# A matmul operand at another place modulo 256 bytes, and unread products in the first wait

## The chip, the cores and the metric

One core of a Trainium2 chip runs the whole program. The metric is the device time of one execution in microseconds (us); lower is better. Six names recur: TensorE (PE, and PEld for its loads of the stationary operand), VectorE (DVE), ScalarE (ACT), GpSimd (POOL), SyncE (SP, which issues most DMAs), and the DMA queues. "Stationary" is the operand that a matmul holds (128 x 128 here), "moving" the one that streams past it.

## What is computed

A trunk of four layers on x, 512 rows of 1024 numbers in float32. Each layer adds a mixer and then an FFN to x, both behind an RMS norm; the mixers are S5 (layers 0 and 3), gated linear attention (1) and differential attention (2). What the change touches most is the FFN, which is the same in all four layers:

```python
def swiglu_ffn(h, w_gate_up, w_down):
    g, u = jnp.split(h @ w_gate_up, 2, axis=-1)
    return (jax.nn.silu(g) * u) @ w_down
...
x = x + swiglu_ffn(h, ffn_w_gate_up[layer], ffn_w_down[layer]).astype(x.dtype)
```

h has 512 rows and 1024 columns, w_gate_up 2 x 2816 columns, w_down is 2816 x 1024.

## The kernel before

**Products in parts.** A float32 operand is split into a high part that TensorE takes in one pass (float32r) and a low rest. ScalarE rounds the high part (L404), VectorE subtracts it (L412), and a product is three single-pass matmuls: high with high, high with low, low with high. The weights' parts lie in the buffers "whl" (pool wp, five buffers of 8192 bytes in each partition).

**The FFN's first half.** The 2816 hidden columns are worked in 11 blocks of 256 (`seven_block`, L580). A block's gate and up columns are computed together with h in the manner of Strassen: seven products of half-size matrices in place of eight. Each product (`seven_product`, L565, its matmul at L575) is 24 matmuls: 2 halves of the output x 4 parts of the contraction x 3 parts. The weights are stationary (128 x 128 from whl), and a "side" of h is moving (256 columns at a time). A side is a tile of 2 x 4 x 256 numbers, 8192 bytes in a partition, made once in each layer: "11", "12", "1", "2", "3", "4" and "22". The steps and their sides and banks are: one (side 11, bank a), five (1, c), six (2, a), two (12, d), seven (3, a), three (4, c), four (22, a). Two is the only one with bank d, which comes from `sbank` (tag "s"); a and c come from `acc`.

**Where the sides lie.** `Sides.room` (L160) takes a tile "sides" of 4096 + 64 numbers from the pool hp (tag hT, two buffers, 16640 and 16384 bytes) and places "11" at number 48 and "12" at number 2112 of it. The other five are tiles of the FFN's own pool (`Sides.open`). The pool wp with whl lies right behind hp. Lines `self.edge(pool, n)` add tiles of n bytes that nothing uses.

**The order in the FFN** (`ffn`, L721). First an opening: blocks 0 and 1 (called a and b) run step by step in an order written out by hand, `plan`, in which the sides are made as well. Then groups: nb blocks, each one, five, six, two, seven, three, four, and behind them the second half, `gemm_b` twice (d = 0, 1), in which the blocks' results ("act") are stationary and w_down's columns move, 512 at a time (L432 to L434). Groups have 4, 4 and 3 blocks in layers 1, 2 and 3, and 3, 3, 3 and 2 in layer 0; the opening's blocks 0 and 1 belong to the first group. In layers 0 and 1 small pieces of other work (`job`) are put between the matmuls of `gemm_b`.

**The kernel's start** (`s5_first`, L1594). The first S5 mixer's tables are computed on VectorE from small inputs while x arrives. TensorE has little to do: it transposes the parameters (L920, L935), then waits for a DMA (craw) for L1141, `s5_qt`, whose result cps VectorE takes at L1160. Behind it stands `warmed(12)`: twelve full-precision products of ident with itself into a bank that nobody reads, which keep TensorE busy until the next transposes (L1038) can run. From the line `self.hand(PE, Activation)` on, the order on TensorE and ScalarE is that of the code. zT, the tile of the mixer's turned outputs, lies idle until the first of them is written.

Of the kernel before, what the change touches and what calls it, by code (L numbers as in the profile page):

```python
# [11 lines left out]
F32 = mybir.dt.float32  # L12
# [9 lines left out]
P = 128  # L22
# [45 lines left out]
class Left:  # L68
# [15 lines left out]
    def room(self):  # L84
        self.hT = [self.tr.hp.tile([P, KT, SEQ], F32R, tag="hT", name=f"hT{z}") for z in range(2)]
# [67 lines left out]
class Sides(Left):  # L153
# [6 lines left out]
    def room(self):  # L160
        F = self.tr.hp.tile([P, 4, 4, 256], F32, tag="hT", name="halves")
        self.whole = F
        self.F = {(0, 0): F[:, 0], (1, 0): F[:, 1], (0, 1): F[:, 2], (1, 1): F[:, 3]}

        two = self.tr.hp.tile([P, 4096 + 64], F32R, tag="hT", name="sides")
        at = lambda n: two[:, n : n + 2048].rearrange("p (z k n) -> p z k n", z=2, k=4)
        self.place = {"11": at(48), "12": at(2112)}
        self.heads = []

    def quarter(self, q, half, b):  # L170
# [154 lines left out]
class Trunk:  # L325
# [254 lines left out]
    def seven_block(self, fp, slots, left, wgu, b, turn, na):  # L580
# [48 lines left out]
        def room1(room=None):  # L629
            load("1", 0, 1, (0, 0), room)  # L630

        def room22(room=None):
            load("22", 1, 1, None, room)
# [87 lines left out]
    def ffn(self, l, left, after=None, turn=False, aside=None, small=None):  # L721
# [7 lines left out]
        with self.tc.tile_pool(name=f"ffn{l}", bufs=1, reuse_waits="tile") as fp:  # L729
# [6 lines left out]
            if glued:  # L736
                lent = room()
# [448 lines left out]
            else:  # L1186
                self.dq.dma_start(d[r, :, g], src[r])

    def warmed(self, n):

        ps = self.sbank("warmed")
        for _ in range(n):
            self.nc.tensor.matmul(ps[:, :P], self.ident[:], self.ident[:], start=True, stop=True)

    def s5_rows(self, nb, bp, Q):

# [397 lines left out]
    def s5_first(self, ctx):  # L1594
        nc, i = self.nc, self.i
        xin = self.xp.tile([P, NT, D], F32, tag="x", name="xin")
        zpool = ctx.enter_context(self.tc.tile_pool(name="zT0", bufs=1, side="right"))
        zT = zpool.tile([P, 2, KT, SEQ], F32R, name="zT")
        self.edge(zpool, 32)
        with self.tc.tile_pool(name="s5_0", bufs=1) as p:  # L1600
            scr, more = (self.hp.tile([P, 4096], F32, tag="hT", name=f"scr{z}") for z in range(2))
            oms = [more[:, 1024 * z : 1024 * z + 1024].rearrange("p (a b) -> p a b", a=2) for z in range(2)]
# [33 lines left out]
            with self.tc.issue_after(self.last_power.ins):  # L1636
                new_x(0)
                X[0][2]()
            self.hand(mybir.EngineType.PE, mybir.EngineType.Activation)
            with self.tc.issue_after(self.last_sine.ins):  # L1640
                ps = self.s5_qt(raw[0][1])
                self.warmed(12)
                hu = self.s5_in(scr, xin, (rounded, rows[0]))
            with self.tc.issue_after(self.last_row.ins):
                X[0][3]()
# [6 lines left out]
            room = [four[:, n] for n in range(4)] + [wide[:, 512:], self.np_.tile([P, 512], F32, tag="R", name="z1", bufs=1)[:]]  # L1652
# [851 lines left out]
```

## Time and profile before

| what | value |
|---|---|
| timed runs, median of 3 | 2278.27 us (2277.72 to 2279.32) |
| the profiled execution, first to last instruction (span) | 2272.3 us |
| granted TensorE clock, mean | 0.996 |

The profile is one execution, taken by the hardware profiler; its page gives the span and no other time of that execution. "Busy" of a group is the time in which at least one of its instructions ran. Matmuls overlap: the mean length of one includes its way through the array, so the pace of a stream is read from where the next one starts. "x24" counts instructions; a full-precision product counts as two matmuls, and a single-pass one as one.

### The profile page before, as it was taken

What the parts mean: (1) busy time and instruction counts of PE and PEld (TensorE: products, weight loads), DVE (VectorE), ACT (ScalarE), POOL (GpSimd) and SP (SyncE); (2) the same over time, 40 slices, a digit from 0 to 9 for tenths busy, and PEclk for the clock granted to TensorE, in tenths of its full rate; (3) what the DMA queues carried; (4) which work ended last, traced back from release to release, by engine and by line L of the source; (5) the groups of instructions that cost most, each with busy time, mean ns of one, the idle gap of its engine ahead of it and who ended that gap; (6) DMA issues with size and microseconds to landing.
All of it is one profiled execution on the core that took longest, in us unless ns stands there. A gap on an engine that the chain in (4) does not pass through costs nothing. (4 is left out here: it accounts for less than half of the span.)

```text
span 2272.3 us, 37257 instructions
## 1 busy us (share of the span) xinstructions
PE 2198.1 (97%) x14871; PEld 1955.4 (86%) x14871; DVE 1584.4 (70%) x2413; ACT 1109.9 (49%) x1779; POOL 328.0 (14%) x446
## 2 busy tenths in 40 slices
PE   6999999999999999999999999999999899999998
PEld 5888889889777799998988887999999888989997
DVE  9965878786525488777745676976766965957675
ACT  6634545454443355554435675644534224635343
POOL 6401142421000010100002231110000000101000
PEclk9999999999999999999999999999999999999999
DMA  4356666663322556665247465985641555766622
GB/s 88 64 171 167 166 157 179 163 180 93 114 76 66 153 154 177 181 172 154 94 139 149 98 148 135 230 213 143 170 100 57 141 155 147 194 172 157 168 75 75
DMA packets 294504, 319.92 MB, mean 141 GB/s; under 512 B 70141, under 2 KB 233241, under 8 KB 294202
## 3 DMA queue, kind: packets, MB, share of 16 engines
q1 hardware_dynamic: 231706, 235.79, 34.1%
q0 software_dynamic: 62624, 81.75, 19.4%
q8 instruction: 117, 1.92, 0.3%
q14 instruction: 57, 0.47, 0.1%
HBM read 285.62 MB, written 16.65 MB: 133 GB/s over the span
## 5 line engine op out<-in xcount | busy, mean ns | idle before, releaser
L412 DVE TENSOR_TENSOR whl<-wst,whl 128x1024 fp32r<-128x1024 f32 x272 | 331.9, 1225 | 267.7 <-ACT whl L404 267.0
L404 ACT CAST whl<-wst 128x1024 fp32r<-128x1024 f32 x272 | 284.5, 1051 | 342.5 <-PE acc L434 242.2
L575 PE MATMUL a<-side,whl 128*128 128x256 f32 x3168 | 383.0, 277 | 6.7 <-DVE whl L412 6.0
L575 PEld LDWEIGHTS a<-side,whl 128*128 128x128 f32 x3168 | 370.2, 188 | 8.9 <-DVE whl L412 6.8
L432 PE MATMUL acc<-whl,act 128*128 128x512 f32 x704 | 278.9, 396 | 1.8 <-DVE g L620 1.6
L433 PE MATMUL acc<-whl,act 128*128 128x512 f32 x704 | 275.7, 392 | 0.0
L434 PE MATMUL acc<-whl,act 128*128 128x512 f32 x704 | 275.7, 392 | 0.0
L575 PE MATMUL c<-side,whl 128*128 128x256 f32 x2112 | 254.8, 277 | 3.6 <-DVE whl L412 3.6
L575 PEld LDWEIGHTS c<-side,whl 128*128 128x128 f32 x2112 | 246.6, 188 | 4.5 <-DVE whl L412 4.4
L412 DVE TENSOR_TENSOR whl<-slot,whl 128x1024 fp32r<-128x1024 f32 x105 | 127.9, 1222 | 64.2 <-ACT whl L404 64.1
L432 PEld LDWEIGHTS acc<-whl,act 128*128 128x128 f32 x704 | 132.6, 188 | 31.7 <-DVE g L620 2.0
L434 PEld LDWEIGHTS acc<-whl,act 128*128 128x128 f32 x704 | 132.5, 188 | 27.9
L433 PEld LDWEIGHTS acc<-whl,act 128*128 128x128 f32 x704 | 132.7, 189 | 26.2 <-issue 0.2
L404 ACT CAST whl<-slot 128x1024 fp32r<-128x1024 f32 x105 | 109.9, 1051 | 74.1 <-PE acc L434 28.2
L432 PE MATMUL acc<-whl,hT 128*128 128x512 f32 x352 | 142.1, 404 | 1.5 <-DVE ro L2233 1.5
L434 PE MATMUL acc<-whl,hT 128*128 128x512 f32 x352 | 137.6, 391 | 0.0
L433 PE MATMUL acc<-whl,hT 128*128 128x512 f32 x352 | 137.4, 390 | 0.0
L575 PE MATMUL d<-sides,whl 128*128 128x256 f32 x1056 | 133.6, 283 | 2.6 <-ACT whl L404 2.6
L575 PEld LDWEIGHTS d<-sides,whl 128*128 128x128 f32 x1056 | 128.9, 191 | 3.4 <-ACT whl L404 3.4
L575 PE MATMUL a<-sides,whl 128*128 128x256 f32 x1056 | 128.9, 278 | 1.7 <-DVE whl L412 1.2
L575 PEld LDWEIGHTS a<-sides,whl 128*128 128x128 f32 x1056 | 124.6, 188 | 3.0 <-DVE whl L412 1.4
L611 POOL DMA_DIRECT2D wst<-in_ffn_w_gate_up_dram x44 | 57.1, 1297 | 442.8 <-DMA wst<-in_ffn_w_gate_up_dram 159.6
(458 smaller groups left out, 3930.0 us busy)
## 6 DMA issues: line engine op xcount, KB each, us to landing
wst<-in_ffn_w_gate_up_dram SPq DMA_DIRECT2D x88, 512.0 KB, 4.4
wst<-in_ffn_w_down_dram SPq DMA_DIRECT2D x88, 512.0 KB, 4.4
slot<-in_ffn_w_gate_up_dram SPq DMA_DIRECT2D x69, 512.0 KB, 6.1
wst<-in_ffn_w_gate_up_dram POOLq DMA_DIRECT2D x44, 512.0 KB, 6.0
halves<-in_ffn_w_gate_up_dram SPq DMA_DIRECT2D x42, 512.0 KB, 5.6
wst<-in_s_w_glu_dram SPq DMA_DIRECT2D x32, 512.0 KB, 4.9
wst<-in_gla_w_in_dram SPq DMA_DIRECT2D x24, 512.0 KB, 3.6
wst<-in_diff_w_qkv_dram SPq DMA_DIRECT2D x24, 512.0 KB, 3.7
```

The costliest lines, as they stand in the source:

```text
L404: self.last["high"] = self.nc.scalar.copy(hl[:, 0], w[:])
L412: self.last["low"] = self.nc.vector.tensor_tensor(hl[:, 1], w[:], hl[:, 0].bitcast(F32), op=ALU.subtract)
L432: mm(out, lh, rh, start=first, stop=False)
L433: mm(out, lh, rl, start=False, stop=False)
L434: self.last["mm"] = mm(out, ll, rh, start=False, stop=last)
L575: mm(o, hl[:, x, k, c], side[:, y, k], start=first and not (j or k or n), stop=k == 3 and n == 2, skip_group_check=True,)
L611: nc.gpsimd.dma_start(w[:], left.quarter(*plus, b), accum_op=ALU.add)
```

## The change

The side "12" begins at number 2096 of the tile "sides" and no longer at 2112; its size and everything that reads or writes it stay. `warmed` gets other products and another place: it runs ahead of `s5_qt` (and no longer behind it), with 14 products of ident, then single-pass products with the stationary operand at 16 places (three products of 256 columns at each, steps of 4 numbers) and at 8 places (three of 512 columns, steps of 8 numbers), all read from zT, whose first 1024 numbers GpSimd sets to zero ahead of the tables. Nobody reads the results.

```diff
-        self.place = {"11": at(48), "12": at(2112)}
+        self.place = {"11": at(48), "12": at(2096)}
...
-    def warmed(self, n):
-
+    def warmed(self, room):
+
+        mm = self.nc.tensor.matmul
         ps = self.sbank("warmed")
-        for _ in range(n):
-            self.nc.tensor.matmul(ps[:, :P], self.ident[:], self.ident[:], start=True, stop=True)
+        for _ in range(14):
+            mm(ps[:, :P], self.ident[:], self.ident[:], start=True, stop=True)
+        for n, step in ((256, 4), (512, 8)):
+            for at in range(512, 576, step):
+                for _ in range(3):
+                    mm(ps[:, :n], room[:, at : at + P], room[:, :n], start=True, stop=True)
...
         self.edge(zpool, 32)
+        unread = zT[:].rearrange("p z k n -> p (z k n)")
+        nc.gpsimd.memset(unread[:, :1024].bitcast(F32), 0.0)
         with self.tc.tile_pool(name="s5_0", bufs=1) as p:
...
             self.hand(mybir.EngineType.PE, mybir.EngineType.Activation)
+            self.warmed(unread)
             with self.tc.issue_after(self.last_sine.ins):
                 ps = self.s5_qt(raw[0][1])
-                self.warmed(12)
                 hu = self.s5_in(scr, xin, (rounded, rows[0]))
```

## The prediction

> **What bounds it.** I read the page's busy times and groups first, then the chain of work that ended last inside one FFN, then stretches of TensorE's products.
>
> ```profile
> PE 2198.1 (97%) x14871; PEld 1955.4 (86%) x14871; DVE 1584.4 (70%) x2413; ACT 1109.9 (49%) x1779; POOL 328.0 (14%) x446
> ...
> L575 PE MATMUL d<-sides,whl 128*128 128x256 f32 x1056 | 133.6, 283 | 2.6 <-ACT whl L404 2.6
> ...
> L575 PE MATMUL a<-sides,whl 128*128 128x256 f32 x1056 | 128.9, 278 | 1.7 <-DVE whl L412 1.2
> ```
>
> TensorE is busy nearly all the time, and its FFN products hardly wait: 2.6 us of idle time stand before all 1056 matmuls of the second product (the only one that writes a bank d). The first product reads the same tile "sides" with the same shapes, yet d is busy 4.7 us longer. Why, the chain shows. Columns: start, length, what; one product is 24 matmuls. This is a group of four blocks of layer 2's FFN, in the order one, five, six, two, seven, three, four, and so on:
>
> ```profile
> 1552.95 2.83 PE a L575 x24
> 1555.78 2.83 PE c L575 x24
> 1558.60 2.83 PE a L575 x24
> 1561.43 2.87 PE d L575 x24
> 1564.30 2.74 PE a L575 x24
> 1567.04 2.72 PE c L575 x24
> 1569.76 5.44 PE a L575 x48
> ...
> 1580.64 2.86 PE d L575 x24
> ```
>
> Two things are to be seen. Each d costs 2.86 where the others cost 2.72 (5.44 for two): 0.14 lost, and 0.02 more in the product behind it (2.74). And the first three products of this group do not run at 2.72 but at 2.83, each of them, until the first d (2.87); behind it the pace is 2.72 for good. So there are two stable paces for the same work on the same places, and d, slow itself, is what brings TensorE from the slow one to the fast one. The next view has the first three products (72 matmuls) of all nine such groups: stretch, length, then busy time of PE. At the fast pace they are 3 x 2.72 = 8.16.
>
> ```profile
> 325.58:333.87 8.29, 8.29 (x73) 8.29 (x73) 1.00 0.70 149
> 424.79:432.97 8.18, 8.18 (x73) 8.18 (x72) 1.00 0.94 169
> 523.39:531.87 8.48, 8.48 (x73) 8.48 (x72) 1.00 0.41 132
> 932.56:940.82 8.26, 8.26 (x72) 8.26 (x73) 1.00 0.65 131
> 1053.43:1061.91 8.48, 8.47 (x72) 8.47 (x72) 1.00 0.36 116
> 1552.79:1561.27 8.48, 8.48 (x73) 8.48 (x72) 1.00 0.72 161
> 1673.45:1681.93 8.48, 8.48 (x72) 8.47 (x72) 1.00 0.36 115
> 2053.44:2061.92 8.48, 8.48 (x72) 8.48 (x72) 1.00 0.69 153
> 2174.11:2182.59 8.48, 8.48 (x73) 8.48 (x72) 1.00 0.37 117
> ```
>
> Six groups enter slow (8.48, which is 3 x 2.827) and hold it through all 72 matmuls; three enter fast after a short settling (8.18 to 8.29).
>
> **The place.** Counted from the sizes in the code, "sides" begins at the same place modulo 256 as the weight buffers whl, which lie 16640 + 16384 = 129 x 256 bytes behind it. "11" is 48 x 4 = 192 bytes on, "12" 2112 x 4 = 33 x 256, so 0 on. Counted in the same way, the five other sides are 192 on, side 1 for one: 68800 = 268 x 256 + 192 bytes behind whl. After the change "12" begins at 2096 x 4 = 32 x 256 + 192: at the distance of the six others. In a group that runs fast, two then costs 2.72 like one: 0.14 + 0.02 = 0.16 less for each block. In a group that enters slow, nothing is left that differs from what held 2.83 for three products over three different sides, so I let the slow pace hold to the group's last product.
>
> For a group of n blocks the cost above 7n x 2.72 is now 3 x 0.107 + 0.15 + 0.02 + (n - 1) x 0.16, and then 7n x 0.107. For n = 4 (at 1552 and 2053): 0.97 becomes 3.00, +2.03. For n = 3 (1053, 1673, 2174): 0.81 becomes 2.25, +1.44. For n = 2 (523): 0.65 becomes 1.50, +0.85. Sum: 2 x 2.03 + 3 x 1.44 + 0.85 = +9.2 us. The three fast groups (10 blocks: 3, 3 and 4) give 10 x 0.16 = -1.6. Five blocks that are done before these groups, behind the last wait of a layer's opening (one in layer 0, two in 1 and 3), give -0.8.
>
> What part of this is on the path? In the chain nothing stands between a group's products, so theirs is whole. The openings (a layer's first two blocks) wait for the splits of weights:
>
> ```profile
> 252.93 5.50 PE L575 MATMUL a<-side,whl 128*128 128x256 f32 x46 [1.74 <-DVE whl L412]
> 262.48 2.86 PE L575 MATMUL c<-side,whl 128*128 128x256 f32 x22 [1.10 <-DVE whl L412]
> 932.56 2.98 PE L575 MATMUL a<-sides,whl 128*128 128x256 f32 x24 [0.45 <-DVE x L558]
> 1500.98 2.21 PE L575 MATMUL a<-side,whl 128*128 128x256 f32 x17 [0.43 <-ACT r L679]
> ```
>
> What two:a and two:b save there, some 2 x 0.14 + 0.02 = 0.3 in each layer, ends in a longer wait of this kind: nothing, and -1.2 for all four layers if that cover is gone. In the same way layer 1's 0.32 of the five blocks ends in the wait at 932.56, and layer 2's blocks 2 and 3 in that at 1500.98. So -0.8 becomes -0.5, and the place is worth 9.2 - 1.6 - 0.5 = +7.1 us.
>
> Here a page speaks against any effect. The Trainium skill, "TensorE: Matmul & The Clock Gate", section "Step-by-step: what each phase is for", says that the two operands come through read ports of their own, so that loading the next weights takes nothing from the running matmul. By that the place of a side is worth 0 and the time stays; 2.86 against 2.72 in this trace does not agree.
>
> **The first wait.** Columns: start, length, engine and line; in brackets the idle time before.
>
> ```profile
> 1.45 0.94 POOL L1016 MEMSET frow<- 128x1024 f32 x1
> 4.65 0.24 POOL L991 IOTA params<- 128x128 int32 x1 [2.26 <-PE s5ps L920]
> 5.16 0.30 PE L935 MATMUL s5ps<-ident,params 24*128 24x24 f32 x1 [0.58 <-DVE params L929]
> 15.98 1.12 PE L1141 MATMUL cps<-ident,craw 128*64 128x128 f32 x8 [10.53 <-DMA craw<-in_s_c_re_dram]
> 18.49 4.73 PE L1193 MATMUL warmed<-ident 128*128 128x128 f32 x24
> 23.36 0.60 PE L1038 MATMUL frow<-ident,params 128*12 128x128 f32 x4
> 24.16 0.27 DVE L1160 TENSOR_SCALAR Q<-cps 64x128 f32<-64x128 f32 x1
> 24.29 0.56 ACT L1039 CAST frow<-frow 12x512 fp32r<-12x512 f32 x1
> 42.71 1.09 PE L1141 MATMUL cps<-ident,craw 128*64 128x128 f32 x16
> ```
> ```profile
> 18.48:22.27 3.79, 3.78 (x17) 3.79 (x18) 1.00 0.00 0
> ```
>
> The added memset has the shape of frow's, 0.94, and lies in GpSimd's idle 2.26. The products move ahead of cps (two times 8 records at 15.98 and 17.43): they can start at 5.5. One product on ident is two records; the first 17 here took 3.79, 0.22 each, the remaining seven 0.95 in all with the last one's drain, so about a half each: TensorE comes to its full clock at about 22.3, 6.3 us after its first matmul at 15.98. Taken over: from 5.5 to 11.8 at half speed, which does 3.1 of the work; the work at full speed is 28 x 0.11 + 48 x 0.113 + 24 x 0.227 = 14.0 (0.227 is twice a fast 256). It ends at 11.8 + 10.9 = 22.7, and cps, 1.1 at full clock, at 23.8. frow's four transposes then come 0.45 late, to 24.4, where ScalarE takes them at 24.29; VectorE takes cps at 24.16, and is busy without a break from there to the clip at 30.28. Cost: 0. Bounds: all at full clock from the start ends at 19.5 and gains nothing, as VectorE sets the pace; all at half speed ends at 5.5 + 28 = 33.5, cps at 35.8, and costs 11.6. I take 0, as the clock did rise in this trace after 6.3 us of such work. The Trainium skill, same page, section "The HAM clock gate", has it rise after a busy window of about 3.4 us that runs freely, so after 3.4 to 6.8; this trace's 6.3 agrees, and the sum stays 0.
>
> **Sum.** +7.1 + 0 on the profiled execution's span of 2272.3 gives 2279.4. The page has no other time of that execution; the median of the timed runs, 2278.27, lies 6.0 above its span. Forecast: 2285.4, 0.31% slower.
>
> **Rivals.** (1) The slow pace ends without the old d: in the first two, or in seven, three or four, which were never seen to enter from it. For it: d always left the fast pace behind. Against: the slow pace never ended by itself in 6 x 72 matmuls. Then only the gains count: 3.1 in the six groups ((0.97 - 0.32) x 2 + 0.49 x 3 + 0.33) and 2.1 elsewhere, -5.2: 2273.1; 2271.2 if the six slow entries (0.32 each) go too. This is the faster side; it is decided at one place, the fourth product of a slow group: if two runs at 2.72 there, the sum turns round. (2) The place is not the cause. d is also the only product whose bank has the tag "s"; then nothing changes: 2278.3. Against it stands a product into a bank with that tag, alo, which runs like one into an acc bank (both 391 ns):
>
> ```profile
> L1938 PE MATMUL alo<-hT,walr 128*32 128x512 f32 x16 | 3.8, 391 | 0.0
> ```
> ```profile
> L434 PE MATMUL acc<-whl,hT 128*128 128x512 f32 x352 | 137.6, 391 | 0.0
> ```
>
> The page's rule of separate ports comes to the same time. (3) The slow pace holds in some groups only: between 2274 and 2284. (4) Worse: the slow pace goes over into the 512-wide matmuls behind it (48 for each block, 19 blocks). At the same ratio, 2.83 to 2.72, 0.227 would be 0.236: 19 x 48 x 0.009 = +8, 2293. Against it: these came out at one pace after every 256-wide stretch here. A clock that stays low through the first wait ends near it as well, 2297.
>
> **Numbers.** Forecast 0.62, its own range 2283.1 (the openings' 1.2 and layer 1's 0.3 not hidden, and 0.8, the spread of the timed runs) to 2288.9 (a fast group of three blocks enters slow, 0.48 + 2.25, and the same spread); (1) 0.18; (2) 0.06; (3) 0.06; (4) 0.08. A measurement of this kernel tells about 0.2%, 4.6 us, from no change. Slower by more: 0.62 + 0.08 + 0.02 of (3) = 0.72; within: 0.06 + 0.04 = 0.10; faster: 0.18. The range leaves out most of (4) and the lower half of (1): 2273 to 2290.
>
> **What would show it.** Right: d at 2.72 in the groups at 325, 424 and 932; 2.83 for each of the 28 products of the group at 1552, and d no longer told apart from its neighbours; the six entries at 8.48; VectorE's Q at 24.2 within 0.5. Wrong: 2.72 behind the first two of a slow group (rival 1), 2.86 left at d (rival 2), steps over 0.23 in L432 to L434 behind a slow group (rival 4), cps after 24.2.

## The result, and the profile after

| | before | after |
|---|---|---|
| timed runs, median of 5 each | 2278.27 us (2276.39 to 2279.85) | 2293.92 us (2289.18 to 2295.86) |
| ratio after to before | | 1.0063, 95% interval 1.0050 to 1.0075 |
| the profiled execution, span | 2272.3 us | 2294.1 us |
| first FFN product of layer 0 begins in it | 216.28 us | 221.79 us |

The change costs 15.65 us (the interval: 11.4 to 17.1), more than twice the forecast's 7.1. The two profiled executions lie further apart than the medians (21.8 us), so a size is taken from the timed runs below and a mechanism from the traces.

The page of the kernel after, busy times and groups of the FFN's products (columns as in the prediction):

```profile
PE 2227.2 (97%) x14947; PEld 1983.2 (86%) x14947; DVE 1584.9 (69%) x2413; ACT 1110.6 (48%) x1779; POOL 327.7 (14%) x447
...
L575 PE MATMUL a<-side,whl 128*128 128x256 f32 x3168 | 391.5, 280 | 8.3 <-DVE whl L412 5.9
...
L575 PE MATMUL a<-sides,whl 128*128 128x256 f32 x1056 | 131.4, 281 | 2.0 <-DVE whl L412 1.2
L575 PE MATMUL d<-sides,whl 128*128 128x256 f32 x1056 | 130.4, 280 | 2.5 <-ACT whl L404 2.5
```

The same rows of before that the prediction did not need are these:

```profile
L575 PE MATMUL a<-side,whl 128*128 128x256 f32 x3168 | 383.0, 277 | 6.7 <-DVE whl L412 6.0
```

d went from 133.6 to 130.4 us: the place did make it faster. But the first product over the same tile (a from sides) went from 128.9 to 131.4 and the three products a over other sides from 383.0 to 391.5, although nothing of theirs was touched and the idle time ahead of them hardly moved. The chain of work inside a group of layer 3 shows how (start, length, what):

```profile
2074.82 2.83 PE c L575 x24
2077.65 2.83 PE a L575 x24
2080.48 2.83 PE d L575 x24
2083.30 2.83 PE a L575 x24
```

d is no longer told apart, and the product behind it, at which before came to 2.72, runs on at 2.83. The first three products of four of the nine groups of after, in the view that the prediction shows of before (stretch, length, busy PE, busy PEld, clock, DMA share, GB/s):

```profile
330.70:339.28 8.58, 8.58 (x72) 8.58 (x73) 1.00 0.76 157
431.58:439.75 8.17, 8.17 (x72) 8.17 (x72) 1.00 0.93 167
...
943.14:951.70 8.56, 8.56 (x73) 8.56 (x73) 1.00 0.65 132
...
2071.84:2080.32 8.48, 8.48 (x73) 8.48 (x73) 1.00 0.71 153
...
```

The six groups that were forecast slow are slow (8.48 each; one of them is shown). Two more are: the group at 330.70 (8.58, in before 8.29) and the one at 943.14 (8.56, in before 8.26). Only the one at 431.58 is fast. By the order of the products' starts, each slow group keeps 2.83 to its last product, and so do parts of two openings, ten products of layer 1 in one row among them (10 x 2.72 would be 27.20):

```profile
870.01:898.28 28.27, 28.27 (x242) 28.23 (x240) 1.00 0.80 212
```

### The profile page after: what moved, and what is told of

Same layout as the page of the kernel before. It is cut to its first block, busy times and chain, and to the rows that moved or that the text cites. A ratio compares the mean times of both kernels' runs of the same rounds, so it can differ in the third digit from the quotient of the medians.

```text
span 2294.1 us, 37410 instructions
## 1 busy us (share of the span) xinstructions
PE 2227.2 (97%) x14947; PEld 1983.2 (86%) x14947; DVE 1584.9 (69%) x2413; ACT 1110.6 (48%) x1779; POOL 327.7 (14%) x447
## 5 line engine op out<-in xcount | busy, mean ns | idle before, releaser
L575 PE MATMUL a<-side,whl 128*128 128x256 f32 x3168 | 391.5, 280 | 8.3 <-DVE whl L412 5.9
L575 PEld LDWEIGHTS a<-side,whl 128*128 128x128 f32 x3168 | 378.2, 189 | 10.5 <-DVE whl L412 6.7
L432 PE MATMUL acc<-whl,act 128*128 128x512 f32 x704 | 277.9, 395 | 1.2 <-DVE g L620 1.2
L434 PE MATMUL acc<-whl,act 128*128 128x512 f32 x704 | 274.7, 390 | 0.0
L575 PE MATMUL c<-side,whl 128*128 128x256 f32 x2112 | 260.2, 280 | 3.3 <-DVE whl L412 3.3
L575 PEld LDWEIGHTS c<-side,whl 128*128 128x128 f32 x2112 | 252.0, 189 | 4.2 <-DVE whl L412 4.1
L432 PEld LDWEIGHTS acc<-whl,act 128*128 128x128 f32 x704 | 132.1, 188 | 30.6 <-DVE g L620 1.7
L434 PEld LDWEIGHTS acc<-whl,act 128*128 128x128 f32 x704 | 132.1, 188 | 27.9
L432 PE MATMUL acc<-whl,hT 128*128 128x512 f32 x352 | 143.3, 407 | 1.0 <-DVE ro L2240 1.0
L434 PE MATMUL acc<-whl,hT 128*128 128x512 f32 x352 | 138.4, 393 | 0.0
L575 PE MATMUL a<-sides,whl 128*128 128x256 f32 x1056 | 131.4, 281 | 2.0 <-DVE whl L412 1.2
L575 PE MATMUL d<-sides,whl 128*128 128x256 f32 x1056 | 130.4, 280 | 2.5 <-ACT whl L404 2.5
```

What stands on the lines that cost most here:

```text
L432: mm(out, lh, rh, start=first, stop=False)
L434: self.last["mm"] = mm(out, ll, rh, start=False, stop=last)
L575: mm(o, hl[:, x, k, c], side[:, y, k], start=first and not (j or k or n), stop=k == 3 and n == 2, skip_group_check=True,)
```

## The experiments

The first theory after the result was in two parts: the place costs about 10 us, since more groups enter slow than in the trace of before, and the first wait about 5.5, as the first FFN product begins that much later. The rivals were that the new products of the wait bring on the slow pace, and that all of it is the place. Ratios are to runs of before on the same chip, with the 95% interval.

**One part alone.** The place: `"12": at(2096)`, `warmed(12)` as before.

> Only the side 12 at number 2096; the twelve products of ident in the first wait as before. Theory (two separate parts, place +10 and first wait +5.5): 2286 to 2290, +8 to +12 on before, one:a of layer 0 begins at 216.3 as in before, and beside the six groups that were forecast slow also the one at 331 in layer 0 and the one at 943 in layer 1 enter at 2.83. Rival 1 (the new products of the first wait are what brings more groups to the slow pace): the six groups alone, 2285.4, with layer 0 at 331 and layer 1 at 943 fast. Rival 2 (all of the +15.65 is the place): 2292 to 2295.

Measured: 2290.47 against 2280.51, ratio 1.0050 (1.0033 to 1.0067). Two of the groups, in the view used above:

```profile
324.51:332.80 8.29, 8.29 (x73) 8.29 (x73) 1.00 0.70 144
...
932.90:941.45 8.55, 8.55 (x72) 8.55 (x73) 1.00 0.66 132
```

The group at 932.90 is slow without any new product in the first wait; the one at 324.51 is fast here. That one is no matter of the first wait either: the run of all distances further below has the same program as this one to the end of layer 2, the old first wait with it, and there the same group is slow:

```profile
327.37:335.97 8.60, 8.60 (x73) 8.60 (x73) 1.00 0.70 150
```

So rival 1 is not needed, and the forecast's list of slow groups was not a fixed one: it differs between two executions of the same instructions. The other part, the first wait:

```diff
-        self.place = {"11": at(48), "12": at(2096)}
+        self.place = {"11": at(48), "12": at(2112)}
```

(against the changed kernel).

> Only the new products of the first wait; the side 12 at number 2112 as before. Theory (two separate parts): +4 to +6 on before, one:a of layer 0 begins at 221.8 as in after and not at 216.3; d stays at 2.86 and the FFN groups take what they take in before. Rival 1 (the new products bring more groups to the slow pace): +5.5 and up to +3 more, with entries of 2.83 in the groups that before entered at 2.72. Rival 2 (all is the place, the start only looks long in one profiled execution): within 1 of before.

Measured: 2281.19 against 2280.51, ratio 1.0001 (0.9993 to 1.0010): no difference. The part of the theory that gave the first wait 5.5 us falls, and its rival 2 stands as far as the wait goes. In the same trace the group at 935.44 entered slow, as in after, and d ended that three products later:

```profile
935.44:943.94 8.50, 8.50 (x72) 8.50 (x73) 1.00 0.66 133
```

A slow entry of this group is thus nothing that the new place makes; the old place only makes it cheap. For the first wait there was a run with more work in it:

```diff
...
                 ps = self.s5_qt(raw[0][1])
+                self.awake(12)
                 hu = self.s5_in(scr, xin, (rounded, rows[0]))
```

(the old twelve products of ident under another name, added to the kernel with the new wait alone).

> As the run with only the new products of the first wait (side 12 at 2112), and the old twelve products of ident again behind cps, so that TensorE has work until the transposes of frow. Theory (the start is late because the granted clock falls in the idle time between the end of the new products at 22 and the transposes near 25, and stays half in several stretches to 70): the clock stays full from 22 to 45, one:a begins at 216.5 to 217.5, the time is 0 to +1.5 on before. Rival (the start is late because VectorE's chain is held by two products of ident ahead of L935, or by the added memset): no better than the run without the twelve, one:a near 221 and +4 to +6.

Measured: 2282.92, ratio 1.0011 (1.0002 to 1.0019). Neither side came out: the clock did stay full from 24 to 36 us (it fell to 0.63 from 36 to 39), but the twelve products stand in the way of the four transposes (L1038 begins at 25.48, and in after at 23.93), and the first FFN product begins at 220.26. It is a little slower, and no remedy for anything.

**Is it distance 0 that ends the slow pace?** Four unread matmuls at the head of each of the nine groups, on the kernel with the place alone (`left.two` is the tile "sides"; its number 64 is at distance 0):

```diff
...
             bank["a"] = self.acc("a")
+            if b in ((4, 8) if na == 4 else (3, 6, 9)):
+                H["11"] = self.halves(W["11"], 4, 256)
+                for _ in range(4):
+                    nc.tensor.matmul(bank["a"][:, :256], H["11"][:, 0, 0, :P], left.two[:, 64:320], start=True, stop=True)
             product("11", "11", bank["a"], True)
```

> Side 12 at number 2096, the old first wait, and ahead of the first product of the first block of each of the nine groups behind gemm_b four matmuls that nobody reads, with the moving operand at distance 0 modulo 256 from whl (inside the tile sides) and the same stationary operand as the product behind them. Theory (products at distance 0 bring TensorE out of the slow pace, and it is their place alone that does so): every group runs at 2.72 from its first or second product on, also those that entered at 2.83; the nine times four matmuls cost 9 x 0.48 = 4.3, what before loses in its groups (5.0 and 1.6, and 0.5 behind the openings) goes: 2275.5, -2.8 on before. Rival (four matmuls are too few, or it takes what follows a whole product d): the groups stay at 2.83, as the run with the place alone plus 4.3: 2290 to 2295.

Measured: 2282.24, ratio 1.0002 (0.9993 to 1.0012). The chain at the head of the four-block group of layer 2 in this run (L647 is the four matmuls, L576 the products):

```profile
1565.63 0.47 PE a L647 x4
1566.10 2.74 PE a L576 x24
1568.84 2.72 PE c L576 x24
1571.56 2.72 PE a L576 x24
```

Four matmuls at distance 0 bring the group to 2.72, with no change in bank or in the products themselves. Eight of the nine groups ran like this. The ninth is slow, 2.83 for each product to its last:

```profile
427.90:436.39 8.49, 8.49 (x73) 8.49 (x74) 1.00 0.99 168
```

It is the group that entered fast in before (424.79), in after (431.58) and in the run of the place alone (423.48): the four matmuls did not fail to end a slow pace there, they stand ahead of one that was not there without them. Its 21 products lose 2.25 at 2.83, part of why the forecast gain of 2.8 did not come; the time of the place is won back and no more. The changed kernel whole with the same four matmuls:

> The changed kernel whole (12 at 2096 and the new first wait) with the four unread matmuls at distance 0 ahead of the first product of each of the nine groups behind gemm_b. Theory (the new first wait adds nothing, the whole of the change's +15.65 is the slow pace of groups): as the kernel with the place and these four matmuls and the old first wait, which was +1.7 on before (ratio 1.0002): -1 to +4 on before. Rival (the new first wait costs some 4 to 5 beside the place, and the run with it alone only had luck): +5 to +8 on before.

Measured: 2280.73 against 2280.17, ratio 1.0002 (0.9994 to 1.0011), the same as without the new wait. The same eight groups are fast and the same one is slow.

**Another product at distance 0.**

```diff
-        self.place = {"11": at(48), "12": at(2112)}
+        self.place = {"11": at(0), "12": at(2096)}
```

> Old first wait; the side 11 at number 0 of the tile sides (distance 0 modulo 256 from whl) and 12 at 2096 (192, like the others): now the first product of each block has the place that 12 had. Theory (a product at distance 0 costs 0.14 and 0.02 behind it, and is what ends the slow pace, wherever it stands in the block): one at 2.86 in all blocks, two at 2.72, and no group is slow behind its first product; the three slow products at the head of six groups go (3 x 0.107 = 0.32 each), so -1.9 on before, within its uncertainty: 2278 to 2281. Rival (the slow pace at the head of a group comes from the 512-wide products ahead and lasts three products whatever one does, or it is bank d and not the place that ends it): groups that entered slow stay slow from one to four, +8 to +12.

Measured: 2277.38 against 2280.17, ratio 0.9984 (0.9975 to 0.9993). Its chain in layer 2:

```profile
1555.57 2.87 PE a L575 x24
1558.45 2.74 PE c L575 x24
1561.18 2.72 PE a L575 x24
```

What was d's (2.86 and 2.74 behind it) is now the first product's, and no group is slow behind it. The bank d has no part in it.

**All distances, by themselves.** Extra products that nobody reads, ahead of the first group of layer 3; per distance 8 matmuls of 512 columns ("wide"), one product ("bench"), four matmuls at distance 0 ("kick"), the product again (number 64 of the tile is at distance 0, each number adds 4 bytes, and number 112 is at distance 192):

```diff
...
+        for n in range(64, 128, 4):
+            stream()
+            product(n)
+            kicks(4)
+            product(n)
+        for k in (1, 2, 3, 4, 6):
+            stream()
+            product(112)
+            kicks(k)
+            product(112)
```

> A measurement of paces by themselves, on the kernel with 12 at 2096 and the old first wait: ahead of the first group of layer 3, products that nobody reads, each in the FFN's form of 24 matmuls: for each of the 16 distances from 0 to 240 bytes (steps of 16) 8 matmuls of 512 columns, one product, 4 matmuls at distance 0, one product; then for 1, 2, 3, 4 and 6 matmuls at distance 0 in that place, at distance 192. Some 155 us more by their own length, so only the steps count. Theory (distance 0 alone stands out): all distances but 0 (and perhaps one neighbour) at 117.8 ns directly behind the 512-wide matmuls and at 113.3 behind the 4 at distance 0; distance 0 at 119 to 120 both times; one or two matmuls at distance 0 leave the slow pace, three or four end it. Rival (a property of 192 alone, or of where the sides of the FFN lie): other distances have steps of their own, and at some of them no 113.3 is seen.

The chain at distances 0, 16, 112 and 192, in this order:

```profile
1988.54 2.87 PE bench L576 x24
1991.40 0.48 PE kick L852 x4
1991.88 2.88 PE bench L576 x24
...
1996.64 2.72 PE bench L576 x24
1999.36 0.48 PE kick L852 x4
1999.83 2.85 PE bench L576 x24
...
2044.75 2.76 PE bench L576 x24
2047.51 0.47 PE kick L852 x4
2047.98 2.78 PE bench L576 x24
...
2084.78 2.73 PE bench L576 x24
2087.52 0.47 PE kick L852 x4
2087.98 2.83 PE bench L576 x24
```

The theory that distance 0 alone stands out falls. At 0 the product settles at 120 ns a matmul both times. At 16 and at 192 it runs fast once and slow once: two paces, and what stands ahead seems to decide which. At 112 both products come to the fast steps of 113 and 114 ns, after 11 and 12 matmuls. At the twelve other distances both lie between 2.81 and 2.88; 2.72 is not seen there. Nor is a kick always a way to the fast pace: behind a fast product at 192, three and six matmuls at distance 0 led to 2.73 again, but four to 2.83 (at the number of one and two a gap of 0.1 us fell into the same place, and they tell nothing). So it is not that distance 0 stands for "fast": it moves TensorE out of the state that it is in, and where it comes out seems to depend on that state and on the number. Four matmuls led from slow to fast ahead of the six groups that are slow in before and after, and from fast to slow twice here and ahead of the group at 427.90.

**Three predictions from that.** 112 showed the fast pace only, so a product there should end the slow pace for less; 16 should end nothing. Each is one line against before, `"11": at(28)` with `"12": at(2096)` (the first product at 112); `"11": at(2096)` with `"12": at(28)` (the fourth product at 112); `"11": at(4)` with `"12": at(2096)` (the first product at 16).

> Old first wait; the side 11 at number 28 of the tile sides (distance 112 modulo 256 from whl), 12 at 2096 (192). Theory (the pace is a state that holds from one matmul to the next; at 192 both 113.3 and 117.8 are stable, at 112 only 113.3 is, since both products measured there came to it within 12 matmuls; so the first product of each block brings TensorE to the fast pace at some 0.04 in place of the 0.14 that distance 0 cost): one at 2.72 to 2.78 in every block, all others at 2.72, no slow group; 36 blocks x 0.1 = 3.6 below the kernel with 11 at distance 0 (-2.8 on before): 2273 to 2276. Rival (the two products at 112 came to 113.3 by the phase in which they happened to begin): groups that enter slow stay slow, +8 to +14 as with all sides at 192.

Measured: 2274.24 against 2280.79, ratio 0.9973 (0.9964 to 0.9983): 6 us faster than before. Its chain in layer 2, and the first three products of a group of layer 1 that had entered slow in before and in after:

```profile
1555.09 2.76 PE a L575 x24
1557.85 2.73 PE c L575 x24
1560.58 2.72 PE a L575 x24
1563.30 2.72 PE d L575 x24
```
```profile
1054.08:1062.28 8.20, 8.20 (x72) 8.20 (x72) 1.00 0.36 104
```

Behind its first product no group has one at 2.83. The product at 112 is not as cheap as was expected, though: behind fast products it takes 2.79, and the one behind it 2.73, so 0.08 in a block and not 0.04.

> Old first wait; the side 12 at number 28 of the tile sides (distance 112 from whl) and 11 at 2096 (192): as before, but with the second product at 112 and not at 0. Theory (112 ends the slow pace as 0 does, and costs less): the first three products of six or seven groups at 2.83, two at 2.74 to 2.78, then 2.72; before loses 0.16 in each block and this one 0.04: 36 x 0.12 = 4.3 less than before, 2274 to 2277. Rival (the state is not left at 112): groups stay slow, +8 to +14.

Measured: 2277.22, ratio 0.9982 (0.9972 to 0.9991), so 3.6 less than before where 4.3 was expected. Slow at the head of seven groups, 2.76 in d, then fast:

```profile
1561.26 2.83 PE c L575 x24
1564.09 2.83 PE a L575 x24
1566.92 2.76 PE d L575 x24
1569.67 2.73 PE a L575 x24
```

> Old first wait; the side 11 at number 4 of the tile sides (distance 16 from whl), 12 at 2096 (192). Theory (at 16 both paces are stable, as at 192: one product measured there ran at 113.3, one at 118.9): nothing ends a slow group, so 6 to 8 groups are slow through all their products, +8 to +14 on before. Rival (what ends the slow pace is any change of distance within a block, whatever it is): no slow group, as with 11 at distance 0 or better, -3 to -6.

Measured: 2295.98, ratio 1.0063 (1.0049 to 1.0076), the same as the changed kernel. All nine groups are slow to their ends, with those that were fast in before (325, 424 and 932) among them:

```profile
326.38:335.00 8.62, 8.62 (x72) 8.62 (x73) 1.00 0.71 156
427.34:435.84 8.50, 8.50 (x72) 8.50 (x72) 1.00 0.94 164
...
938.90:947.36 8.46, 8.46 (x73) 8.46 (x73) 1.00 0.66 132
```

The time came out as the theory had it, but 16 does more than end nothing. In layer 1's opening (start, length with the last matmul's drain, what; the pace is the step from one start to the next) a product at 16 (from sides) stands behind one that ran at 2.72:

```profile
872.39 2.88 PE L575 MATMUL a<-side,whl 128*128 128x256 f32 x24
875.11 2.96 PE L575 MATMUL a<-sides,whl 128*128 128x256 f32 x24
877.91 2.99 PE L575 MATMUL c<-side,whl 128*128 128x256 f32 x24
880.74 1.46 PE L575 MATMUL a<-side,whl 128*128 128x256 f32 x11
```

It took 2.80, and the one behind it 2.83. There the product at 16 moved TensorE from the fast pace to the slow one, which may be why the groups that were fast in before are slow here.

**The changed kernel with one number mended**, `"11": at(28)` in place of `at(48)`:

> The changed kernel with one number more changed: the side 11 at number 28 (distance 112 from whl) in place of 48; 12 at 2096 and the new first wait stay. Theory (the whole of the change's +15.65 is the slow pace of groups, which 112 ends, and the new first wait is worth nothing): no slow group, and the time of the kernel with 11 at 112 and the old first wait, ratio 0.9973 on before: 2273 to 2276. Rival (the new first wait costs its own 2 to 5 us, which the spread of the kernels with slow groups hid): ratio 0.998 to 1.0, 2277 to 2281.

Measured: 2275.79 against 2280.92, ratio 0.9972 (0.9962 to 0.9982). With the new first wait and with the old one the ratio is the same, 0.9972 and 0.9973, so within about 2 us the whole of the change's cost is the slow pace, and the wait is worth nothing.

## Why the prediction was wrong

**What bounds the kernel, and the mechanism: right.** Two stable paces, d as what brought TensorE from one to the other, and the place, not the bank, as what made d so: all of it came out, in after and in the runs with one part alone or another side at distance 0. Rival 1 (the slow pace ends by itself) fell with the 2.83 behind d, rival 2 (the place isn't the cause) with the first product at distance 0, rival 3 (slow in some groups only) with the eight slow groups of after, which keep 2.83 to their ends, and rival 4 with the groups of the 512-wide matmuls, which are no longer than before in their means (L432 to L434, the rows with act: 395, 390, 390, in before 396, 392, 392).

**A slow group's price: right.** From the first product of a group to that of the next, the four-block groups took 120.66 (layer 2) and 120.67 (layer 3) in before and take 122.67 and 122.66 in after: +2.01 and +1.99, where +2.03 was forecast.

**Which groups are slow: this step failed.** The prediction took the entries of one profiled execution for a property of the kernel and let "the three fast groups (10 blocks: 3, 3 and 4) give 10 x 0.16 = -1.6". The entry is a state at one place in time. In the seven traces that have the first side at 192 and no four matmuls ahead of the groups, the six groups that were forecast slow are slow every time and the one at 424 is fast every time; but the one at 325 is slow in two, and the one at 932 in five, among them one with the old place and three with the old wait. In before a wrong guess about it is worth 0.32, since d ends it; with all sides at 192 it is worth the whole group. By the prediction's own numbers a three-block group that enters slow costs 2.25 more than one that enters fast, and a four-block one 3.00 more. (The top of the range took 0.48 + 2.25 for this; the 0.48 that before loses is in the forecast already, so 2.25 is right.) With the one group more that the run of the place alone had, 7.1 + 3.0 = 10.1, and that run measured 9.96 (ratio 1.0050). With the two of after, 7.1 + 2.25 + 3.0 = 12.35, inside the measured 11.4 to 17.1. With all three, as in the run at distance 16, 7.1 + 2 x 2.25 + 3.0 = 14.6, and 15.2 was measured. The range had room for one such group, not for all of them.

The traces bear this out as a whole. The lengths of the nine groups, from the first product to the first matmul of `gemm_b`, summed in the one trace of each kernel and taken against before, make +12.7 in after, +10.5 with the place alone and +15.4 with the first side at 16, -2.0 with it at 0, -4.7 with it at 112, and -2.3 with the fourth product at 112. The timed runs have +15.65, +9.96, +15.2, -2.8, -6.6 and -3.6.

**The openings: mis-sized, the other way.** With the place alone the openings of layers 0, 1 and 3, from first product to `gemm_b`, took 0.55, 0.64 and 0.65 less, 1.8 together where 0.5 was forecast: the waits for the splits did not take these gains back. (Layer 2's opening took 0.5 to 3.6 more than in before in every other trace, with the old places too, and tells nothing.) In after 14 slow products of two openings (14 x 0.107 = 1.5) cancel most of it.

**The first wait: a cost of 0 was forecast, and none was measured, but that is luck.** The working did not hold. The new products begin at 4.44 and not at 5.5, and come to full steps soon after 9 and not at 11.8 (15 matmuls fall in 6 to 9 us, 26 in 9 to 12). Such steps are all that the full clock was read from, in the prediction too: the granted clock is 1.00 in these rows of either trace. They end at 21.65, where 22.7 was worked out. But VectorE takes cps at 25.79 and not at 24.2, the sign that the prediction named: its steps ahead of that are 0.58 late (L1033 at 23.70, in before at 23.12), and another instruction goes first. Two of the unread products stand ahead of L935 (5.59, in before 5.16), which may account for it; no run shows that. TensorE then has little to do from 22.7 to 27, and the granted clock falls. The rows of after and of before, from 24 to 30 us (columns as above, all engines):

```profile
24.00:27.00 3.00, 1.71 (x8) 0.97 (x9) 2.90 (x7) 3.00 (x4) 2.43 (x4) 0.90 0.30 33
27.00:30.00 3.00, 3.00 (x38) 2.51 (x37) 2.96 (x5) 1.65 (x4) 2.84 (x6) 0.54 0.00 0
```
```profile
24.00:27.00 3.00, 1.48 (x10) 0.84 (x12) 2.86 (x8) 2.97 (x5) 2.11 (x5) 1.00 0.20 22
27.00:30.00 3.00, 2.98 (x42) 2.39 (x43) 3.00 (x4) 2.45 (x5) 2.92 (x5) 1.00 0.00 0
```

This looked like the cause of the 5.5 us by which the first FFN product is later. But a fall is not the new wait's alone, and does not fix the start: the run with the four matmuls and the old wait has one at the same place and its first product at 219.27, and the run of all distances (old wait, 0.57 from 27 to 30) has it at 216.58.

```profile
27.00:30.00 3.00, 3.00 (x36) 2.59 (x35) 3.00 (x4) 1.82 (x4) 2.92 (x5) 0.55 0.00 0
```

Over the profiled executions here (without the one with the extra twelve products), the first FFN product begins between 215.93 and 219.27 with the old wait and between 217.94 and 221.79 with the new one, by the medians 2.4 later. The timed runs, many more, tell no difference: with the new wait alone they lie between 1.6 less and 2.3 more than before. So no cost is shown, and one of up to 2 us is not excluded.

The Trainium skill, "TensorE: Matmul & The Clock Gate", section "The HAM clock gate", has the activity window run freely, so that one kernel shows another number of slow matmuls from run to run. These traces agree where the start is the same: of the eight with the old wait two have a granted clock of 0.55 and 0.57 from 27 to 30 us, and six have 1.00. With the new wait all four have a fall there (0.54 to 0.63), so that seems to be more than chance. On the Trainium skill's same page, "Step-by-step: what each phase is for" has the two operands read through ports of their own, from which the prediction took that the place would be without effect; the ratio 1.0050 with the side 12 moved from 0 to 192 and nothing else does not agree with that.

**The sum** stood on the median of three runs, 2278.27; further runs of before had medians of 2280 to 2281, and the profiled execution (2272.3) was a short one. That moved nothing in the ratio.

What stays open: why the pace depends on the distance, why a fast one was seen just at 16, 112 and 192, and what decides in which state a group is entered. The weights' buffers never moved, so the runs do not tell the distance between the operands from the place of the moving operand alone. No run here looks inside TensorE's reads.

## What to carry to other kernels

Where one profile shows the same instructions at two paces, ask which of the two is stable and what moves the one to the other, and price the change for the case that every entry falls on the wrong side: an instruction that looks merely slow can be the one that keeps the rest fast. Do not take a state seen in one execution for a property of the kernel; look at it in a second execution, or in variants that should not differ in it. And a late start in one trace is no cost until timed runs of that part alone show it.

## What the runs showed of the hardware

In streams that wait for nothing, the pace of single-pass products of 256 columns went with the place of the moving operand modulo 256 bytes, counted here from the stationary one, which never moved: 113.3 ns a matmul at best (2.72 for 24), 117 to 120 at most places (2.81 to 2.88). At 192 bytes two paces hold, each for dozens of matmuls on end. At 16 one product ran at 113.3 ns and the other at 119, and in the kernel a product there led from the fast pace to the slow one. At 112 both products came to the fast pace after 11 or 12 matmuls; at 0 the pace is 120. With one side at 112 and the six others at 192 the whole kernel takes 0.27% less than with one at 0 and six at 192 (0.9973, 0.9964 to 0.9983), and with all seven at 192 0.50% more (1.0050, 1.0033 to 1.0067).
